# A decoder layer on one core: the state-space tables moved from GpSimd to VectorE, by sums and differences of angles

## The chip, the cores and the metric

The kernel runs on one core of a Trainium2 chip. The metric is device time in microseconds (us) of one execution, as the median of several runs; lower is better. The core has five engines that run their own instruction queues and wait for each other by semaphores: TensorE (PE; PEld is its loading of weights), VectorE (DVE), ScalarE (ACT), GpSimd (POOL) and SyncE (SP), which here only starts transfers from memory.

## What is computed

One layer of a decoder on a sequence of 256 positions and 2048 channels, in float32. Three token mixers run in parallel on one projection `h = x @ W_in`: a diagonal complex state-space model (S5), and two gated linear attentions (GLA and HGRN2). Their outputs are projected up, gated and summed, then comes an output projection, a layer norm, a squared-ReLU MLP with 8192 hidden channels and a second layer norm. The change touches S5 alone:

```python
dt = exp(log_dt); mag = exp(lr * dt)               # 64 groups, 64 states each
abar = mag * (cos(li * dt) + i sin(li * dt))
bu = einsum('bsgc,gpc->bsgp', ug, bbar)            # complex; 16 channels a group
s_t = abar * s_{t-1} + bu_t                        # scan over 256 positions
y = Re(einsum('bsgp,gcp->bsgc', s, c)) + d * ug
```

## The kernel before, in words

**The main stream.** Nearly all work is big matrix products on TensorE. To keep float32 accuracy with a faster operand type, each operand is split into a high part (rounded, by ScalarE, line 129) and a low part (operand minus high part, by VectorE, line 107); a product is then three matmuls, or two where a 256-column operand holds both parts side by side (lines 1341 to 1343, and 1346 and 1347). The weights stream from memory through SP's queue in tiles of 512 KB, 128 partitions by 1024 elements, fetched up to 8 tiles ahead (`AHEAD`). Each tile is split shortly before use: `emit_split` gives ScalarE the high part, `emit_lower` gives VectorE the low part, a 128x1024 subtraction. So TensorE needs one such subtraction for every tile, and a tile lasts two *steps*; a step is six matmuls of 512 columns, or eight of 512 and 256 alternating.

**The side tasks.** All else (S5, the attentions, norms) is written as generators that are woken between steps. The order on each engine is that in which the Python code issues instructions; nothing reorders it later. `run_tasks(vb, sb)` (called at line 1318) is the pacing: every instruction on VectorE or ScalarE issued through the helpers adds its estimated time to a counter, every step takes 1240 ns off, and tasks of lower priority go on only while both counters are negative. `yield n` puts a task to sleep for about 2n steps. GpSimd's instructions are not counted.

**S5.** `s5_params` prepares, for each of 64 groups' states, angle steps, and pages `sn` and `cs` with sine and cosine of fine angles (time 0 to 15) and coarse ones (16 times 0 to 15). The work then goes through 16 *half blocks* of 4 groups, in two pairs of 128 states:
- `s5_prepare` (line 432) sets up, per block of two half blocks, masked copies of B and C (`EB`, `EC`, lines 444 and 445), transposes them on TensorE into `W`, and stacks u and B three times on 96 partitions by transfers on SP (`RU`, `RB`); then ScalarE rounds the stacks to high parts, and VectorE subtracts on the 32 partitions that are to hold low parts.
- `s5_tables` (line 484) makes, for a half block, sine and cosine of all 256 times from fine and coarse angles by the addition theorem: six products or sums of 128x512 on GpSimd (lines 493 to 498).
- `s5_main` (line 502) multiplies the stacks (`pb`, line 519), rotates the result by the tables so that the recurrence becomes real (products that read PSUM, 128x256 each, one per pair and part), scans it (line 543, four scans of 128x256), rotates back, and multiplies by C (line 563).

The attentions (`attention`, line 605) work by levels, each with products on TensorE that need VectorE's last result (line 634). Their two large factors are multiplied once before level 0. GpSimd otherwise only fills one page per attention with zeros and starts small transfers at the beginning.

Of the kernel before, what the change touches and what calls it, by code (L numbers as in the profile page):

```python
# [8 lines left out]
F32 = mybir.dt.float32  # L9
# [46 lines left out]
def trunk_kernel(ctx: ExitStack, tc, io, out):  # L56
# [48 lines left out]
    def tt(o, a, b, op):  # L105
        used["v"] += size(o) / 0.96 + 80
        V.tensor_tensor(o, a, b, op=op)  # L107
# [170 lines left out]
    def s5_params():  # L278
# [153 lines left out]
    def s5_prepare():  # L432


        yield from wait_for("par")
        EB, EC = S5["EB"], S5["EC"]
        b4 = S5["B"].rearrange("q r (j c) -> q r j c", j=32)
        c4 = S5["C"].rearrange("r i (b p) -> r i b p", b=8)
        for b in range(8):
            for g in range(2):  # L440
                h = slice(64 * g, 64 * g + 64)
                for ri in range(2):
                    used["v"] += 120
                    V.tensor_copy(EB[h, ri, :, g, :], b4[h, ri, 4 * b:4 * b + 4, :])
                ts(EC[:, :, g, :], c4[:, :, b, :], S5["gm"][:, g:g + 1], None, ALU.mult)
            yield 4
            yield from wait_for(("u", b // 4))
            yield from room("hf", 1, 4)
            ps = psm()
            transposes(ps, [EB[:, ri].rearrange("q j g c -> q (j g c)") for ri in range(2)] +  # L450
                       [EC[:, ri].rearrange("r g p -> r (g p)") for ri in range(2)])
            W = half((128, 4, 128))
            act(W, ps.rearrange("p (b s) -> p b s", b=4), AF.Copy)
            S5["W", b] = W
            yield 1
            u = uT[b // 4][:, b % 4, :]
            for hb in (2 * b, 2 * b + 1):
                yield from room("hf", 4, 4)
                RU, RB = half((96, 2, 256)), half((96, 2, 256))
                for i in range(2):  # L460
                    r = slice(32 * (2 * (hb % 2) + i), 32 * (2 * (hb % 2) + i) + 32)
                    for k in range(3):
                        nc.sync.dma_start(RU[32 * k:32 * k + 32, i, :], u[r])
                        nc.sync.dma_start(RB[32 * k:32 * k + 32, i, :], W[r, 0:2, :].rearrange("p a b -> p (a b)"))
                yield 3
                SU, SB = half((96, 2, 256), F32R), half((96, 2, 256), F32R)
                act(SU, RU, AF.Copy)
                act(SB, RB, AF.Copy)
# [14 lines left out]

    def s5_tables(hb):

        def fine(x):
            return x[:, 0, 2 * hb:2 * hb + 2, :].unsqueeze(2).to_broadcast([128, 2, 16, 16])

        def coarse(x):
            return x[:, 1, 2 * hb:2 * hb + 2, :].unsqueeze(3).to_broadcast([128, 2, 16, 16])  # L490
        sn, cs = S5["sn"], S5["cs"]
        so, co, w = (half((128, 2, 16, 16)) for _ in range(3))
        G.tensor_tensor(co, coarse(cs), fine(cs), op=ALU.mult)
        G.tensor_tensor(w, coarse(sn), fine(sn), op=ALU.mult)
        G.tensor_tensor(co, co, w, op=ALU.subtract)
        G.tensor_tensor(so, coarse(sn), fine(cs), op=ALU.mult)
        G.tensor_tensor(w, coarse(cs), fine(sn), op=ALU.mult)
        G.tensor_tensor(so, so, w, op=ALU.add)
        free(w)
        S5["tab", hb] = tuple(x.rearrange("p i a b -> p i (a b)") for x in (so, co)), (so, co)  # L500

    def s5_main():
        yps = None
        yield from wait_for("par")
        yield from room("hf", 4)
        s5_tables(0)
        for hb in range(16):
            b, off = hb // 2, 2 * (hb % 2)
            u = uT[b // 4]
            (sn, cs), tabs = S5.pop(("tab", hb))  # L510
            while ("stack", hb) not in S5:
                yield 1
            W = S5["W", b]
            SU, SB = S5.pop(("stack", hb))
            uid[0] += 1
            pb = [psa.tile([128, 2, 256], F32, tag="m2", bufs=2, name=f"pb{uid[0]}_{i}") for i in range(2)]
            for i in range(2):
                for ri in range(2):
                    T.matmul(pb[i][:, ri, :], lhsT=SB[:, i, ri * 128:(ri + 1) * 128], rhs=SU[:, i, :],  # L519
                             start=True, stop=True)  # L520
            free(SU, SB)
            if hb + 1 < 16:
                yield from room("hf", 3, 4)
                s5_tables(hb + 1)
            yield from room("hf", 3, 3)
            zr, zi, w1 = half(), half(), half()
            for i in range(2):
                tt(zr[:, i, :], pb[i][:, 0, :], cs[:, i, :], ALU.mult)
                tt(w1[:, i, :], pb[i][:, 1, :], sn[:, i, :], ALU.mult)
            yield 0  # L530
            tt(zr, zr, w1, ALU.add)
            for i in range(2):
                tt(zi[:, i, :], pb[i][:, 1, :], cs[:, i, :], ALU.mult)
            yield 0
            for i in range(2):
                tt(w1[:, i, :], pb[i][:, 0, :], sn[:, i, :], ALU.mult)
            tt(zi, zi, w1, ALU.subtract)
            yield 0
            for z in (zr, zi):
                for i in range(2):  # L540
                    j = 2 * hb + i
                    used["v"] += 340
                    V.tensor_tensor_scan(z[:, i, :], S5["mag"][:, j:j + 1].to_broadcast([128, 256]),  # L543
                                         z[:, i, :], 0.0, ALU.mult, ALU.add)
# [757 lines left out]
    for s, (c, ku, j, t) in enumerate(steps):  # L1302
# [105 lines left out]
```

## Time and profile before

| | |
|---|---|
| median of 3 runs | 1694.33 us (1694.15 to 1695.88) |
| the profiled execution's own time | 1696.22 us |
| its span, first to last instruction | 1694.4 us |
| busy: PE, DVE, ACT, POOL | 1671.3, 1190.8, 825.5, 161.3 us |
| mean granted clock of TensorE | 0.996 |
| GpSimd's table operations | 96, starting between 75.9 and 699.7 us |
| read from memory | 308.71 MB, 183 GB/s over the span |

How to read the rows that follow: a group's row gives the line of the code, the engine, the operation, the tiles written and read with their shapes (partitions x elements), the count, then busy time in us and the mean duration of one in ns, then idle time of that engine just before them with what ended it. Nearly all VectorE instructions go through one helper at line 107 and ScalarE's through line 129, so they are told apart by tiles and shapes: `pg` is a page of 1024 elements per partition, `hf` a half page of 512, `acc`, `pb` and `m` are PSUM banks. Successive instructions of one engine overlap a little, so a group's busy time over its count is less than the mean duration. A row of the timeline starts with the start and the duration in us; x2 means two instructions in a row, and the duration is that of both. A busy PE includes matmuls whose modelled ends overlap.

### The profile page before, as it was taken

Reading aid. Unit: us, or ns where it says so; the run is one execution under the profiler, and the core shown is the slowest. Engines: PE = TensorE matmul, PEld = TensorE weight load, DVE = VectorE, ACT = ScalarE, POOL = GpSimd, SP = SyncE. Lnnn points to the kernel's source line nnn. Section 1 sums busy time; section 2 is a strip of 40 time slices with the busy share of each in tenths; the row PEclk is TensorE's granted clock in tenths of the full one; section 3 lists DMA queues with packets and bytes.
Section 4 is the critical chain, followed back from the end, with each engine's and each line's share of the span. In section 5 each row is a group of like instructions: output and inputs, shape, how many; then the busy total and the mean of one; then the engine's idle time right before and its main releaser. Section 6 shows DMA issues by size and latency. Waiting matters only on the chain.

```text
span 1694.4 us, 24226 instructions
## 1 busy us (share of the span) xinstructions
PE 1671.3 (99%) x9396; PEld 1386.1 (82%) x9396; DVE 1190.8 (70%) x1587; ACT 825.5 (49%) x1166; POOL 161.3 (10%) x121
## 2 busy tenths in 40 slices
PE   9999999999999999999999999999999999999997
PEld 7887788887877877788888888888888888888886
DVE  6968778797998999985575667545555545555556
ACT  5553554564644434435554466454454545464550
POOL 3222022012332332200000000000000000000000
PEclk9999999999999999999999999999999999999999
DMA  9945655564555665676676545655656565656561
GB/s 287 275 145 157 178 177 168 153 194 139 173 180 169 194 196 172 207 221 186 200 263 220 187 150 150 197 188 187 211 179 206 163 213 171 218 163 208 197 233 50
DMA packets 222900, 318.70 MB, mean 188 GB/s; under 512 B 13205, under 2 KB 122129, under 8 KB 222785
## 3 DMA queue, kind: packets, MB, share of 16 engines
q1 hardware_dynamic: 217488, 308.59, 58.3%
q10 hardware_dynamic: 4528, 7.31, 1.3%
q0 software_dynamic: 768, 1.25, 0.5%
q8 instruction: 74, 1.21, 0.3%
q14 instruction: 42, 0.34, 0.1%
HBM read 308.71 MB, written 2.10 MB: 183 GB/s over the span
## 4 chain that ended last, share of the span: by engine, by line
PE 66%; DVE 4%; issue 1%; ACT 0%; DVEq 0%
PE acc L1341 15%; PE acc L1342 15%; PE acc L1343 15%; PE acc L1346 14%; PE acc L1347 7%; DVE pg L107 2%; DVE hf L107 1%; PE m L134 1%; DVE hf L543 1%; PE m L563 1%; DVE pg L118 0%; PE pb L519 0%; ACT pg L129 0%; DVE st L941 0%; DVEq L1403 0%
## 5 line engine op out<-in xcount | busy, mean ns | idle before, releaser
L129 ACT ACTIVATE pg<-pg 128x1024 fp32r<-128x1024 f32 (+2 forms) x604 | 603.1, 1028 | 413.7 <-PE acc L1342 147.0
L107 DVE TENSOR_TENSOR pg<-pg,pg 128x1024 fp32r<-128x1024 f32 (+3 forms) x646 | 749.9, 1188 | 58.9 <-ACT pg L129 32.7
L1341 PE MATMUL acc<-pg,pg 128*128 128x512 f32 x1504 | 595.5, 396 | 2.7 <-DVE pg L107 1.8
L1342 PE MATMUL acc<-pg,pg 128*128 128x512 f32 x1504 | 587.3, 390 | 2.7 <-DVE pg L107 2.7
L1343 PE MATMUL acc<-pg,pg 128*128 128x512 f32 x1504 | 587.0, 390 | 0.2
L1346 PE MATMUL acc<-pg,pg 128*128 128x512 f32 x1552 | 551.9, 400 | 0.0
L1347 PE MATMUL acc<-pg,pg 128*128 128x256 f32 x1552 | 436.6, 281 | 1.9 <-DVE pg L107 1.9
L1346 PEld LDWEIGHTS acc<-pg,pg 128*128 128x128 f32 x1552 | 292.4, 188 | 72.9 <-issue 0.7
L1341 PEld LDWEIGHTS acc<-pg,pg 128*128 128x128 f32 x1504 | 282.8, 188 | 68.4 <-issue 5.8
L1343 PEld LDWEIGHTS acc<-pg,pg 128*128 128x128 f32 x1504 | 282.6, 188 | 61.5 <-DVE pg L107 1.4
L1342 PEld LDWEIGHTS acc<-pg,pg 128*128 128x128 f32 x1504 | 282.9, 188 | 60.6 <-DVE pg L107 5.1
L1347 PEld LDWEIGHTS acc<-pg,pg 128*128 128x128 f32 x1552 | 293.9, 189 | 2.8 <-DVE pg L107 2.3
L129 ACT ACTIVATE hf<-acc 128x256 f32<-128x256 f32 (+2 forms) x103 | 40.0, 388 | 184.5 <-PE acc L1347 179.6
L107 DVE TENSOR_TENSOR pg<-pg,acc 128x512 f32<-128x512 f32 x56 | 38.3, 685 | 121.3 <-PE acc L1343 121.3
L107 DVE TENSOR_TENSOR hf<-acc,hf 128x256 f32<-128x256 f32 (+1 forms) x69 | 29.1, 421 | 131.9 <-ACT hf L129 131.9
L107 DVE TENSOR_TENSOR hf<-hf,hf 128x512 f32<-128x512 f32 (+1 forms) x144 | 106.6, 758 | 4.7 <-ACT hf L129 2.8
L129 ACT ACTIVATE hf<-hf 128x256 f32<-128x256 f32 (+1 forms) x152 | 67.7, 456 | 2.3 <-DMA hf<-pg 0.5
L129 ACT ACTIVATE pg<-acc 128x512 f32<-128x512 f32 x40 | 23.8, 595 | 83.7 <-PE acc L1343 74.5
L107 DVE TENSOR_TENSOR hf<-pb,hf 128x256 f32<-128x256 f32 x128 | 46.5, 414 | 22.8 <-PE pb L519 16.8
L107 DVE TENSOR_TENSOR pg<-hf,pg 128x256 fp32r<-128x256 f32 x84 | 34.7, 421 | 27.7 <-ACT pg L129 27.6
L129 ACT ACTIVATE pg<-m 128x512 fp32r<-128x512 f32 (+2 forms) x35 | 19.6, 559 | 68.0 <-PE m L134 51.8
L543 DVE TENSOR_TENSOR_SCAN hf<-p,hf 128x256 f32<-128x256 f32 x64 | 47.7, 792 | 0.0
(128 smaller groups left out, 641.1 us busy)
## 6 DMA issues: line engine op xcount, KB each, us to landing
pg<-in_w_in_dram SPq DMA_DIRECT2D x224, 512.0 KB, 4.2
pg<-in_w_mlp_in_dram SPq DMA_DIRECT2D x128, 512.0 KB, 4.6
pg<-in_w_mlp_out_dram SPq DMA_DIRECT2D x128, 512.0 KB, 4.0
pg<-in_w_up_dram SPq DMA_DIRECT2D x48, 512.0 KB, 4.7
pg<-in_w_out_dram SPq DMA_DIRECT2D x32, 512.0 KB, 5.5
pg<-in_s_w_glu_dram SPq DMA_DIRECT2D x8, 512.0 KB, 4.7
hf<-pg SPq DMA_DIRECT2D x96, 32.0 KB, 1.9
hf<-hf SPq DMA_DIRECT2D x96, 32.0 KB, 1.9
```

The costliest lines, as they stand in the source:

```text
L107: V.tensor_tensor(o, a, b, op=op)
L129: S.activation(o, a, f, **kw)
L134: T.transpose(ps[:, i * 128:(i + 1) * 128], s, ident)
L543: V.tensor_tensor_scan(z[:, i, :], S5["mag"][:, j:j + 1].to_broadcast([128, 256]), z[:, i, :], 0.0, ALU.mult, ALU.add)
L563: T.matmul(yps[r, 0:256], lhsT=W[:, 2 + ri, r], rhs=m[:, i, :], start=ri == 0, stop=ri == 1)
L1341: T.matmul(ps, lhsT=a[0][:, sl], rhs=wh[:, i, :], start=f, stop=False)
L1342: T.matmul(ps, lhsT=a[0][:, sl], rhs=wl[:, i, :], start=False, stop=False)
L1343: T.matmul(ps, lhsT=a[1][:, sl], rhs=wh[:, i, :], start=False, stop=l)
L1346: T.matmul(ps, lhsT=wh[:, i, n], rhs=a[2], start=f, stop=False)
L1347: T.matmul(ps[:, 0:256], lhsT=wl[:, i, n], rhs=a[0], start=False, stop=l)
```

## The change

- The time vector's fine part is moved by a half (0.5 to 15.5), and the tables no longer come from all 16 fine angles but from the first 8: with coarse angle c and fine angle f, cos(c ± f) and sin(c ± f) share the same four products, so 8 fine angles give 16 times, 8 by the sum and 8, in reverse order, by the difference. A table now takes four operations of 128x256 (two products, a sum, a difference); sine and cosine together take eight. They are issued on VectorE, through the counted helper, with a `yield 0` after each pair. GpSimd has none of them.
- `pb` holds a part (real or imaginary) of both pairs in one bank rather than both parts of one pair, so each rotation product covers both pairs: four products of 128x512 per half block instead of eight of 128x256.
- u and B are split before they are stacked, on all 128 partitions, once per block: ScalarE rounds u and B to high parts (two copies of 128x256; the copy of C's half shrinks to 128x256), VectorE makes two subtractions of 128x256. The transfers on SP, as many and as large as before, pick the high or low part. The subtractions on 32 partitions are gone.
- The pacing takes 1290 ns off per step instead of 1240.

```diff
+        ts(tvec[:, 0, :], tvec[:, 0, :], 0.5, None, ALU.add)
...
-            yield from room("hf", 1, 4)
+            yield from room("hf", 3, 4)
+            u = uT[b // 4][:, b % 4, :]
+            UP = half((128, 2, 256), F32R)
+            act(UP[:, 0, :], u, AF.Copy)
...
-            W = half((128, 4, 128))
-            act(W, ps.rearrange("p (b s) -> p b s", b=4), AF.Copy)
+            W, BP = half((128, 2, 128)), half((128, 2, 256), F32R)
+            act(BP[:, 0, :], ps[:, 0:256], AF.Copy)
+            act(W, ps[:, 256:512].rearrange("p (b s) -> p b s", b=2), AF.Copy)
             S5["W", b] = W
+            yield 0.5
+            tt(UP[:, 1, :], u, UP[:, 0, :].bitcast(F32), ALU.subtract)
+            tt(BP[:, 1, :], ps[:, 0:256], BP[:, 0, :].bitcast(F32), ALU.subtract)
             yield 1
...
-                        nc.sync.dma_start(RU[32 * k:32 * k + 32, i, :], u[r])
-                        nc.sync.dma_start(RB[32 * k:32 * k + 32, i, :], W[r, 0:2, :].rearrange("p a b -> p (a b)"))
+                        nc.sync.dma_start(RU[32 * k:32 * k + 32, i, :], UP[r, int(k == 1), :].bitcast(F32))
+                        nc.sync.dma_start(RB[32 * k:32 * k + 32, i, :], BP[r, int(k == 2), :].bitcast(F32))
...
-                yield 0.5
-                tt(SU[32:64], RU[32:64], SU[32:64].bitcast(F32), ALU.subtract)
-                tt(SB[64:96], RB[64:96], SB[64:96].bitcast(F32), ALU.subtract)
...
-        so, co, w = (half((128, 2, 16, 16)) for _ in range(3))
-        G.tensor_tensor(co, coarse(cs), fine(cs), op=ALU.mult)
-        G.tensor_tensor(w, coarse(sn), fine(sn), op=ALU.mult)
-        G.tensor_tensor(co, co, w, op=ALU.subtract)
-        G.tensor_tensor(so, coarse(sn), fine(cs), op=ALU.mult)
-        G.tensor_tensor(w, coarse(cs), fine(sn), op=ALU.mult)
-        G.tensor_tensor(so, so, w, op=ALU.add)
-        free(w)
+        so, co = half((128, 2, 16, 16)), half((128, 2, 16, 16))
+        for o, x1, y1, x2, y2, op1, op2 in ((co, cs, cs, sn, sn, ALU.subtract, ALU.add),
+                                            (so, sn, cs, cs, sn, ALU.add, ALU.subtract)):
+            w = half((128, 2, 2, 16, 8))
+            tt(w[:, 0], coarse(x1), fine(y1), ALU.mult)
+            tt(w[:, 1], coarse(x2), fine(y2), ALU.mult)
+            yield 0
+            tt(o[:, :, :, 8:16], w[:, 0], w[:, 1], op1)
+            tt(o[:, :, :, 7::-1], w[:, 0], w[:, 1], op2)
+            free(w)
+            yield 0
...
-                    T.matmul(pb[i][:, ri, :], lhsT=SB[:, i, ri * 128:(ri + 1) * 128], rhs=SU[:, i, :],
+                    T.matmul(pb[ri][:, i, :], lhsT=SB[:, i, ri * 128:(ri + 1) * 128], rhs=SU[:, i, :],
...
-            for i in range(2):
-                tt(zr[:, i, :], pb[i][:, 0, :], cs[:, i, :], ALU.mult)
-                tt(w1[:, i, :], pb[i][:, 1, :], sn[:, i, :], ALU.mult)
+            tt(zr, pb[0], cs, ALU.mult)
+            tt(w1, pb[1], sn, ALU.mult)
...
-        run_tasks(1240, 1240)
+        run_tasks(1290, 1290)
```

The order of VectorE's instructions moves at three places. The first is where the tables of the first half block are made, about 87 to 93 us into the trace. `pg_829`, `pg_859` and, after the change, `pg_835`, `pg_866` and `pg_899` are low parts of successive weight tiles; `s5eb` and `s5ec` are the masked copies for `s5_prepare`; `hf_884` and `hf_911` hold products of sines and cosines, `hf_883` and `hf_882` the two tables. Before:

```order
L107 TENSOR_TENSOR pg_829<-pg_621,pg_828 128x1024
L107 TENSOR_TENSOR pg_733<-acc_765,hf_861 128x256
L444 COPY s5eb<-pg_188 64x4x16 x2
L112 TENSOR_SCALAR s5ec<-pg_189,gmask 128x2x64
L444 COPY s5eb<-pg_188 64x4x16 x2
L112 TENSOR_SCALAR s5ec<-pg_189,gmask 128x2x64
L107 TENSOR_TENSOR pg_859<-pg_651,pg_858 128x1024
```

After:

```order
L445 COPY s5eb<-pg_188 64x4x16 x2
L112 TENSOR_SCALAR s5ec<-pg_189,gmask 128x2x64
L107 TENSOR_TENSOR pg_835<-pg_619,pg_834 128x1024
L107 TENSOR_TENSOR pg_735<-acc_769,hf_868 128x256
L107 TENSOR_TENSOR hf_884<-pg_578 128x256
L107 TENSOR_TENSOR hf_884<-pg_577 128x256
L107 TENSOR_TENSOR hf_883<-hf_884 128x32x8 x2
L107 TENSOR_TENSOR pg_866<-pg_649,pg_865 128x1024
L107 TENSOR_TENSOR hf_911<-pg_577,pg_578 128x256
L107 TENSOR_TENSOR hf_911<-pg_578,pg_577 128x256
L107 TENSOR_TENSOR hf_882<-hf_911 128x32x8 x2
L107 TENSOR_TENSOR pg_899<-pg_675,pg_898 128x1024
```

The masked copies come one weight tile earlier, and one table (four operations) now stands ahead of each of two weight tiles' low parts; `pg_866` is the counterpart of `pg_859`.

The second place is the start of the GLA attention, about 143 to 151 us. `pg_1385`, `pg_1416` and, after, `pg_1398`, `pg_1436` are low parts of weights, `hf_1456` and `hf_1476` the attention's diagonal, and the last row is the product on which level 0 waits (`pg_1287`, `pg_1298`). Before:

```order
L112 TENSOR_SCALAR s5ec<-pg_189,gmask 128x2x64
L107 TENSOR_TENSOR pg_1385<-pg_1133,pg_1384 128x1024
L118 SCALAR_TENSOR_TENSOR pg_1287<-acc_1326,hf_1418 128x256
L107 TENSOR_TENSOR hf_1372<-hf_1372,hf_1232 128x512
L107 TENSOR_TENSOR hf_904<-hf_904,hf_1231 128x512
L107 TENSOR_TENSOR pg_1416<-pg_1165,pg_1415 128x1024
L107 TENSOR_TENSOR hf_1456<-m_1458,dg 128x256
L107 TENSOR_TENSOR pg_1287<-pg_1287,pg_978 128x1024
```

After:

```order
L118 SCALAR_TENSOR_TENSOR hf_883<-hf_883,hf_882 128x512
L107 TENSOR_TENSOR pg_1398<-pg_1147,pg_1397 128x1024
L118 SCALAR_TENSOR_TENSOR pg_1298<-acc_1337,hf_1438 128x256
L107 TENSOR_TENSOR hf_1413<-pg_507,hf_1413 128x256
L107 TENSOR_TENSOR hf_1421<-m_1415,hf_1421 128x256
L107 TENSOR_TENSOR pg_1436<-pg_1205,pg_1435 128x1024
L107 TENSOR_TENSOR hf_1476<-m_1478,dg 128x256
L107 TENSOR_TENSOR pg_1298<-pg_1298,pg_1003 128x1024
```

The rotation back of a half block (two 128x512) has moved ahead, and two new subtractions of a block's u and B (`hf_1413`, `hf_1421`) stand in its place; no table operation is near.

The third is the start of a half block late in S5, where `pb` is read. Before (the last half block):

```order
L107 TENSOR_TENSOR pg_7167<-pg_7040,pg_7166 128x1024
L107 TENSOR_TENSOR hf_7208<-pb_0_7202,hf_6946 128x256
L107 TENSOR_TENSOR hf_7210<-pb_0_7202,hf_6945 128x256
L107 TENSOR_TENSOR hf_7208<-pb_1_7203,hf_6946 128x256
L107 TENSOR_TENSOR hf_7210<-pb_1_7203,hf_6945 128x256
L107 TENSOR_TENSOR hf_7208<-hf_7208,hf_7210 128x512
L107 TENSOR_TENSOR hf_7209<-pb_0_7202,hf_6946 128x256
L107 TENSOR_TENSOR hf_7209<-pb_1_7203,hf_6946 128x256
L107 TENSOR_TENSOR pg_7190<-pg_7042,pg_7189 128x1024
```

After (a half block of the same stretch that makes the next one's tables):

```order
L107 TENSOR_TENSOR hf_5875<-pg_578 128x256
L107 TENSOR_TENSOR hf_5875<-pg_577 128x256
L107 TENSOR_TENSOR hf_5874<-hf_5875 128x32x8 x2
L107 TENSOR_TENSOR pg_5836<-pg_5730,pg_5835 128x1024
L107 TENSOR_TENSOR pg_5839<-m_5890,pg_5838 128x4x128
L107 TENSOR_TENSOR hf_5903<-pg_577,pg_578 128x256
L107 TENSOR_TENSOR hf_5903<-pg_578,pg_577 128x256
L107 TENSOR_TENSOR pg_5888<-pg_5750,pg_5887 128x1024
L107 TENSOR_TENSOR hf_5873<-hf_5903 128x32x8 x2
L107 TENSOR_TENSOR hf_5928<-pb_0_5867,hf_5596 128x512
L107 TENSOR_TENSOR hf_5930<-pb_1_5868,hf_5595 128x512
L107 TENSOR_TENSOR pg_5914<-pg_5773,pg_5913 128x1024
```

The tables' eight operations stand ahead of the first products from `pb`, with weights' low parts between them; the products are fewer and longer. On GpSimd the 96 table operations are gone from the order, and its zero fills and first transfers stay.

More of the change, by code (lines that the diff above doesn't have):

```diff
@@ L451, in s5_prepare @@
                        [EC[:, ri].rearrange("r g p -> r (g p)") for ri in range(2)])
-            W = half((128, 4, 128))
-            act(W, ps.rearrange("p (b s) -> p b s", b=4), AF.Copy)
+            W, BP = half((128, 2, 128)), half((128, 2, 256), F32R)
+            act(BP[:, 0, :], ps[:, 0:256], AF.Copy)
+            act(W, ps[:, 256:512].rearrange("p (b s) -> p b s", b=2), AF.Copy)
             S5["W", b] = W
+            yield 0.5
+            tt(UP[:, 1, :], u, UP[:, 0, :].bitcast(F32), ALU.subtract)
+            tt(BP[:, 1, :], ps[:, 0:256], BP[:, 0, :].bitcast(F32), ALU.subtract)
             yield 1
-            u = uT[b // 4][:, b % 4, :]
             for hb in (2 * b, 2 * b + 1):
@@ L468, in s5_prepare @@
                 act(SB, RB, AF.Copy)
-                yield 0.5
-                tt(SU[32:64], RU[32:64], SU[32:64].bitcast(F32), ALU.subtract)
-                tt(SB[64:96], RB[64:96], SB[64:96].bitcast(F32), ALU.subtract)
                 free(RU, RB)
-                yield 1.5
+                yield 1
                 S5["stack", hb] = SU, SB
+            free(UP, BP)
     SIN2 = 6.2831845
@@ L486, in fine @@
         def fine(x):
-            return x[:, 0, 2 * hb:2 * hb + 2, :].unsqueeze(2).to_broadcast([128, 2, 16, 16])
+            return x[:, 0, 2 * hb:2 * hb + 2, 0:8].unsqueeze(2).to_broadcast([128, 2, 16, 8])
         def coarse(x):
-            return x[:, 1, 2 * hb:2 * hb + 2, :].unsqueeze(3).to_broadcast([128, 2, 16, 16])
+            return x[:, 1, 2 * hb:2 * hb + 2, :].unsqueeze(3).to_broadcast([128, 2, 16, 8])
         sn, cs = S5["sn"], S5["cs"]
-        so, co, w = (half((128, 2, 16, 16)) for _ in range(3))
-        G.tensor_tensor(co, coarse(cs), fine(cs), op=ALU.mult)
-        G.tensor_tensor(w, coarse(sn), fine(sn), op=ALU.mult)
-        G.tensor_tensor(co, co, w, op=ALU.subtract)
-        G.tensor_tensor(so, coarse(sn), fine(cs), op=ALU.mult)
-        G.tensor_tensor(w, coarse(cs), fine(sn), op=ALU.mult)
-        G.tensor_tensor(so, so, w, op=ALU.add)
-        free(w)
+        so, co = half((128, 2, 16, 16)), half((128, 2, 16, 16))
[9 more added lines that the diff above has]
+            yield 0
         S5["tab", hb] = tuple(x.rearrange("p i a b -> p i (a b)") for x in (so, co)), (so, co)
@@ L505, in s5_main @@
         yield from room("hf", 4)
-        s5_tables(0)
+        yield from s5_tables(0)
         for hb in range(16):
@@ L523, in s5_main @@
                 yield from room("hf", 3, 4)
-                s5_tables(hb + 1)
+                yield from s5_tables(hb + 1)
             yield from room("hf", 3, 3)
             zr, zi, w1 = half(), half(), half()
-            for i in range(2):
-                tt(zr[:, i, :], pb[i][:, 0, :], cs[:, i, :], ALU.mult)
-                tt(w1[:, i, :], pb[i][:, 1, :], sn[:, i, :], ALU.mult)
+            tt(zr, pb[0], cs, ALU.mult)
+            tt(w1, pb[1], sn, ALU.mult)
             yield 0
             tt(zr, zr, w1, ALU.add)
-            for i in range(2):
-                tt(zi[:, i, :], pb[i][:, 1, :], cs[:, i, :], ALU.mult)
+            tt(zi, pb[1], cs, ALU.mult)
             yield 0
-            for i in range(2):
-                tt(w1[:, i, :], pb[i][:, 0, :], sn[:, i, :], ALU.mult)
+            tt(w1, pb[0], sn, ALU.mult)
             tt(zi, zi, w1, ALU.subtract)
@@ L562, in s5_main @@
                 for ri, m in ((0, sre), (1, cs)):
-                    T.matmul(yps[r, 0:256], lhsT=W[:, 2 + ri, r], rhs=m[:, i, :],
+                    T.matmul(yps[r, 0:256], lhsT=W[:, ri, r], rhs=m[:, i, :],
                              start=ri == 0, stop=ri == 1)
```

## The prediction

> **What bounds the kernel now.** I read the page's first part, then busy time by stage, then PE's idle gaps with what ended them, then VectorE's and GpSimd's rows around those gaps.
>
> ```profile
> span 1694.4 us, 24226 instructions
> PE 1671.3 (99%) x9396; PEld 1386.1 (82%) x9396; DVE 1190.8 (70%) x1587; ACT 825.5 (49%) x1166; POOL 161.3 (10%) x121
> ```
>
> TensorE is the bound: 1671.3 of 1694.4 us. The change gives TensorE no less work, so all it can win is where PE waits. In the stages of 50 us below the columns are length, then busy us (and instructions) of PE, PEld, DVE, ACT, POOL, then the granted clock.
>
> ```profile
> 50.00:100.00 50.00, 48.07 (x261) 40.79 (x261) 44.17 (x56) 20.99 (x29) 18.71 (x12) 0.97 0.73 214
> 100.00:150.00 50.00, 47.93 (x322) 40.51 (x320) 38.74 (x53) 30.68 (x38) 10.18 (x8) 1.00 0.53 167
> 150.00:200.00 50.00, 48.98 (x559) 38.99 (x560) 35.75 (x55) 19.80 (x27) 0.00 (x0) 0.97 0.54 159
> 500.00:550.00 50.00, 48.39 (x221) 38.04 (x220) 45.32 (x60) 21.82 (x23) 14.20 (x9) 1.00 0.58 173
> 600.00:650.00 50.00, 48.13 (x223) 38.39 (x222) 45.46 (x63) 21.11 (x24) 12.63 (x9) 1.00 0.51 155
> ```
>
> PE's idle time here is 1.93 + 2.07 + 1.02 = 5.02 us early and 1.61 + 1.87 = 3.48 us in two late stages. Everything the change touches runs between about 60 and 760 us. The two early gaps also cost clock. The next rows are four stretches of 3.41 us in the same columns: for each early gap the one that holds it and the one after.
>
> ```profile
> 89.74:93.15 3.41, 1.48 (x9) 1.03 (x8) 3.40 (x5) 0.41 (x1) 1.60 (x2) 1.00 0.00 0
> 93.15:96.56 3.41, 3.41 (x13) 2.93 (x12) 3.41 (x5) 0.00 (x0) 2.39 (x1) 0.50 0.48 130
> 147.76:151.17 3.41, 0.43 (x20) 0.16 (x21) 3.41 (x4) 0.00 (x0) 2.12 (x1) 1.00 0.32 77
> 151.17:154.58 3.41, 3.41 (x70) 2.88 (x64) 3.41 (x6) 0.00 (x0) 0.00 (x0) 0.50 0.61 171
> ```
>
> After each gap TensorE runs 3.41 us at clock 0.50, which loses 1.7 us: 3.4 us for both. So at most 5.02 + 3.48 + 3.4 = 11.9 us is to be had.
>
> **Who makes PE wait.** The first gap: PE's row with the idle time before it, then VectorE's (start, duration); the last row, from elsewhere, is a measure:
>
> ```profile
> 92.69 0.39 PE L1347 MATMUL acc<-pg,pg 128*128 128x256 f32 x1 [1.93 <-DVE pg L107]
> 87.83 0.28 DVE L444 COPY s5eb<-pg 64x64 f32<-64x64 f32 x2
> 88.03 1.10 DVE L112 TENSOR_SCALAR s5ec<-pg,gmask 128x128 f32<-128x128 f32 x1
> 89.14 1.08 DVE L444 COPY s5eb<-pg 64x64 f32<-64x64 f32 x2
> 90.23 1.26 DVE L112 TENSOR_SCALAR s5ec<-pg,gmask 128x128 f32<-128x128 f32 x1
> 91.42 2.35 DVE L107 TENSOR_TENSOR pg<-pg,pg 128x1024 fp32r<-128x1024 f32 x2
> 142.94 0.29 DVE L112 TENSOR_SCALAR s5ec<-pg,gmask 128x128 f32<-128x128 f32 x1
> ```
>
> PE waits for the low part of a weight tile (the 128x1024 subtraction). VectorE reaches it late because the small operations ahead of it ran beside GpSimd's tables: TENSOR_SCALAR 1.10 and 1.26 us against 0.29 alone (142.94), the pair of copies 1.08 against 0.28. That is 0.81 + 0.97 + 0.80 = 2.6 us. The second gap has the same shape:
>
> ```profile
> 139.35 1.11 DVE L444 COPY s5eb<-pg 64x64 f32<-64x64 f32 x2
> 140.38 1.08 DVE L112 TENSOR_SCALAR s5ec<-pg,gmask 128x128 f32<-128x128 f32 x1
> 141.48 1.44 DVE L444 COPY s5eb<-pg 64x64 f32<-64x64 f32 x2
> 144.61 2.15 DVE L107 TENSOR_TENSOR hf<-hf,hf 128x512 f32<-128x512 f32 x2
> 146.68 2.08 DVE L107 TENSOR_TENSOR pg<-pg,pg 128x1024 fp32r<-128x1024 f32 x1
> 151.01 0.98 PE L634 MATMUL m<-pg,pg 128*32 128x16 f32 x64 [2.98 <-DVE pg L107]
> ```
>
> Against the same measures the copies and the s5ec operation lost 0.83 + 0.79 + 1.16 = 2.8 us, the pair of 512-element products 0.8 (2.15 where two at the late 0.66, worked out below, take 1.3) and the subtraction 0.9 (2.08 against 1.19): 4.5 us for a gap of 2.98. The longest gap of the late stage:
>
> ```profile
> 631.03 3.18 DVE L543 TENSOR_TENSOR_SCAN hf<-p,hf 128x256 f32<-128x256 f32 x2
> 636.59 0.50 PE L1342 MATMUL acc<-pg,pg 128*128 128x512 f32 x1 [1.87 <-DVE pg L107]
> ```
>
> Two scans took 3.18 us beside GpSimd; two at the late 0.63 us (below) take 1.3: 1.9 us, the whole gap.
>
> **The change, part by part, on VectorE.** The groups by shape (count | busy us, mean ns | idle before), first of 60 to 745 us, where GpSimd works, with one of ScalarE, then of 745 to 1640, where GpSimd does nothing:
>
> ```profile
> L107 DVE TENSOR_TENSOR pg<-pg,pg 128x1024 fp32r<-128x1024 f32 x218 | 281.7, 1304 | 2.1 <-ACT pg L129 1.7
> L107 DVE TENSOR_TENSOR hf<-hf,hf 128x512 f32<-128x512 f32 x105 | 78.7, 772 | 0.9
> L543 DVE TENSOR_TENSOR_SCAN hf<-p,hf 128x256 f32<-128x256 f32 x60 | 45.2, 800 | 0.0
> L107 DVE TENSOR_TENSOR hf<-pb,hf 128x256 f32<-128x256 f32 x123 | 44.7, 414 | 22.8 <-PE pb L519 16.8 <-issue 6.0
> L107 DVE TENSOR_TENSOR hf<-hf,hf 32x512 fp32r<-32x512 f32 x32 | 23.3, 730 | 3.7 <-ACT hf L129 2.8
> L129 ACT ACTIVATE hf<-acc 128x256 f32<-128x256 f32 x28 | 10.7, 382 | 50.3 <-PE acc L1347 49.5
> ```
> ```profile
> L107 DVE TENSOR_TENSOR pg<-pg,pg 128x1024 fp32r<-128x1024 f32 x323 | 383.8, 1220 | 29.2 <-ACT pg L129 24.3 <-PE acc L1342 2.9 <-issue 0.9
> L107 DVE TENSOR_TENSOR pg<-pg,acc 128x512 f32<-128x512 f32 x47 | 32.2, 685 | 107.0 <-PE acc L1343 107.0
> L107 DVE TENSOR_TENSOR hf<-hf,hf 128x512 f32<-128x512 f32 x7 | 4.6, 683 | 0.1
> L543 DVE TENSOR_TENSOR_SCAN hf<-p,hf 128x256 f32<-128x256 f32 x4 | 2.5, 676 | 0.0
> L107 DVE TENSOR_TENSOR hf<-pb,hf 128x256 f32<-128x256 f32 x7 | 2.6, 416 | 0.0
> ```
>
> *GpSimd's tables go.* By busy time, 218 subtractions cost 281.7 − 218 × 383.8/323 = 22.7 us more than late ones, 105 products 78.7 − 105 × 4.6/7 = 9.7, 60 scans 45.2 − 60 × 2.5/4 = 7.7: VectorE gets back 40.1 us; the other groups, the s5ec and s5eb ones above among them, come on top. Products that read PSUM keep their time (414 and 416 ns), so it is two SBUF operands that collide.
>
> The Trainium skill (SBUF — State Buffer, Who interferes with whom) says that a VectorE instruction with two SBUF inputs, or a copy or tensor_scalar in a two-port mode, locks against a GpSimd instruction that reads SBUF, and the loser blocks for the other's whole length. The rows agree in kind (PSUM products untouched, 0.29 us drawn out to 1.1); a loss of all GpSimd time would by this page exceed the 40.1 us that the groups show, and the groups decide.
>
> *Tables on VectorE:* 8 operations of 128x256 per half block, 128 in all. Nearest row: the 128x256 products, 44.7/123 = 0.363 us back to back, 46.5 us; alone 0.414 each, 53.0. I take 46.5, since they stand in pairs. *Rotations:* 128 of 128x256 (46.5 us) become 64 of 128x512 reading PSUM, 64 × 0.685 = 43.8: −2.7. *Low parts of u and B:* 32 of 32x512 (23.3 us) become 16 of 128x256 (5.8): −17.5. The added half step on the time vector is one operation on 16 columns, nothing.
>
> Net on VectorE: 46.5 − 40.1 − 2.7 − 17.5 = −13.8 us. The bounds are +32.8 (tables at 53.0 and nothing given back: 53.0 − 2.7 − 17.5) and −29 (the 16 s5ec operations giving back 0.97 each, 15.5 more).
>
> *Others.* ScalarE gets three copies of 128x256 for one of 128x512 in each of 8 blocks, at most 24 × 0.382 = 9.2 us over 700, and is busy 49% of the time: hidden. If it were full, that would be the price. SP issues the same 192 stack transfers, now behind VectorE's subtraction instead of ScalarE's copy, and weight loads queue behind them on SP; those are issued up to 8 tiles ahead, two steps each, so a wait of a step or two is hidden. Without that cover PE would wait for a tile. PE's matmuls are the same in number and size.
>
> *At the gaps.* First: the order puts half the tables (4 × 0.363 = 1.5 us) ahead of the subtraction that was late. The small operations alone give back 2.6, so 1.1 of 1.93 us; the rest has to come from the work before 87 us, which ran beside another set of GpSimd's products:
>
> ```profile
> 80.97 2.08 DVE L107 TENSOR_TENSOR pg<-pg,pg 128x1024 fp32r<-128x1024 f32 x1
> 83.31 2.92 DVE L107 TENSOR_TENSOR pg<-pg,hf 128x512 f32<-128x512 f32 x2
> ```
>
> These two rows give back 0.9 and 1.6 us more (2.08 against 1.19, 2.92 against 1.3). I take the gap as gone. Second: by the order no table operation stands near the late product, only the two new subtractions of a block (2 × 0.363 = 0.7 us); 4.5 − 0.7 = 3.8 us come back for 2.98. Gone. With both gaps the 3.4 us of half clock go: 5.02 + 3.4 = 8.4. Late stage: the causes go, but 8 × 0.363 = 2.9 us of tables stand at each half block's start and the task budget per step rises from 1240 to 1290 ns, so I take three quarters of 3.48, 2.6. Sum: 8.4 + 2.6 = 11.0 us.
>
> The profiled execution took 1696.22 us, its span 1694.4; from it 1685.2. It is 1.89 above the median of the runs, so for the median 1694.33 − 11.0 = **1683.3 us**.
>
> **Rivals.**
> 1. *VectorE becomes the bound* (slower). If GpSimd gives nothing back, VectorE gets 32.8 us more over 16 half blocks, 2.05 each. From 450 to 700 it has 18.06 us idle:
>
> ```profile
> 450.00:700.00 250.00, 246.17 (x1131) 196.47 (x1130) 231.94 (x311) 112.52 (x128) 70.43 (x48) 1.00 0.59 186
> ```
>
> Some 8 half blocks fall there, 16.4 us: it would be full, its idle time now being waits for others, and PE would wait for most of it: 1694.3 + 16.4 = 1710.7. It decides where less than 32.8 us come back; 40.1 are shown. Chance 0.04.
> 2. *The half clock stays.* If the two slow stretches come by themselves, only 11.0 − 3.4 = 7.6 is won: 1686.7. Against it: in both cases the stretch just before had PE busy 1.48 and 0.43 of 3.41 us. Chance 0.10. The Trainium skill (TensorE: Matmul & The Clock Gate, Part 1) has the clock halve after an idle window of about 3.4 us; by that rule gaps of 1.93 and 2.98 would be too short, and this rival's 1686.7 would hold. The trace speaks against the rule's length.
> 3. *The waits move.* Tables and first products stand together at each half block's start, 8 × 0.363 + 4 × 0.685 = 5.6 us where 2.9 stood. If that costs PE a microsecond in each of 8 half blocks, the late stage loses 8 instead of 3.5: 1694.3 − 8.4 + 4.5 = 1690.4. Against: the code yields after each pair. Chance 0.14.
> 4. *One early gap stays*, because the tables eat what the collision gave back: 2.98 + 1.7 less, 1688.0. Chance 0.08. That the change doesn't do what it says is excluded for GpSimd, on which the order has no product left; that its products have nothing to do with PE's waits, about 1694: 0.02.
>
> **The numbers.** My forecast has 0.62. A fifth of a per cent, 3.4 us, is what a measurement can tell from no change: below 1690.9 counts as faster. Faster: 0.62 + 0.10 + 0.08 + half of rival 3 = 0.87; within: 0.09; slower 0.04. The range runs from 1680.0 (all 11.9 us, 1682.4, less some 2 us of spread as between profile and median) to 1690.4, rival 3; rival 1 and the last are left out.
>
> **What would show it.** No GpSimd products; the 128x1024 subtraction near 1.19 us of busy time and scans near 0.63 before 745; PE idle below 1 us from 50 to 200 and clock 1.00 throughout; VectorE busy below 605 us from 60 to 760. A gap of over 1 us at PE ended by VectorE in 50 to 700, or a 0.50 clock there, proves a step wrong; a VectorE busy over 47 of 50 us for several stages means rival 1 or 3.

## The result, and the profile after

The changed kernel takes 1682.84 us (median of 4 runs, 1682.36 to 1683.05), the kernel before in the same session 1695.11: a ratio of 0.9924, 95% interval 0.991 to 0.9937. The forecast was 1683.3. The profiled execution took 1682.36 us against 1696.22, 13.9 less. Most executions of the kernel before took about 1694.3 us with a mean granted clock of 0.997, or about 1696.1 us with 0.996. The page of after:

```profile
span 1680.6 us, 24111 instructions
PE 1665.3 (99%) x9396; PEld 1384.1 (82%) x9396; DVE 1159.6 (69%) x1636; ACT 828.8 (49%) x1183; POOL 15.6 (1%) x25
```

By stage (length, then busy us and instructions of PE, PEld, DVE, ACT, POOL, then the clock), the five stages shown of before and the two long ones:

```profile
50.00:100.00 50.00, 50.00 (x284) 42.90 (x283) 40.95 (x68) 23.75 (x34) 0.00 (x0) 1.00 0.72 212
100.00:150.00 50.00, 48.60 (x445) 41.38 (x445) 40.45 (x64) 31.18 (x40) 0.96 (x1) 1.00 0.63 191
150.00:200.00 50.00, 50.00 (x448) 39.97 (x448) 40.62 (x61) 22.83 (x29) 0.00 (x0) 1.00 0.60 172
500.00:550.00 50.00, 50.00 (x233) 40.09 (x232) 46.34 (x73) 23.95 (x28) 0.00 (x0) 1.00 0.57 167
600.00:650.00 50.00, 50.00 (x231) 40.05 (x230) 43.86 (x66) 21.42 (x25) 0.00 (x0) 1.00 0.65 202
450.00:700.00 250.00, 250.00 (x1152) 201.70 (x1151) 221.88 (x337) 115.39 (x140) 0.00 (x0) 1.00 0.62 189
60.00:760.00 700.00, 698.60 (x4622) 572.05 (x4621) 579.94 (x902) 346.60 (x481) 2.89 (x3) 1.00 0.60 181
```

PE's idle time from 50 to 200 us went from 5.02 to 1.40, in the late stages to nothing, and the granted clock is 1.00 throughout these rows. VectorE is busy 579.9 of 700 us instead of 605.4, though it does the tables now. Its groups from 60 to 745 us (count | busy us, mean ns | idle before):

```profile
L107 DVE TENSOR_TENSOR pg<-pg,pg 128x1024 fp32r<-128x1024 f32 x223 | 269.3, 1217 | 4.7 <-ACT pg L129 2.8 <-issue 1.9
L107 DVE TENSOR_TENSOR hf<-hf,hf 128x512 f32<-128x512 f32 x109 | 72.0, 684 | 0.8
L107 DVE TENSOR_TENSOR hf<-pb,hf 128x512 f32<-128x512 f32 x64 | 42.4, 683 | 7.8 <-PE pb L528 7.8
L549 DVE TENSOR_TENSOR_SCAN hf<-p,hf 128x256 f32<-128x256 f32 x64 | 39.4, 671 | 0.0
L107 DVE TENSOR_TENSOR hf<-hf 128x256 f32<-128x256 f32 x64 | 24.3, 421 | 0.6
L107 DVE TENSOR_TENSOR hf<-pg,pg 128x256 f32<-128x256 f32 x32 | 12.1, 418 | 0.0
L107 DVE TENSOR_TENSOR hf<-pg 128x256 f32<-128x256 f32 x32 | 12.0, 417 | 0.0
L445 DVE COPY s5eb<-pg 64x64 f32<-64x64 f32 x32 | 4.6, 184 | 0.1
L112 DVE TENSOR_SCALAR s5ec<-pg,gmask 128x128 f32<-128x128 f32 x16 | 4.5, 279 | 0.1
```

The large groups with two SBUF operands are back at the durations that the kernel before has only after 745 us: subtractions 1217 ns (1304 before the change), scans 671 (800), products 684 (772). The tables are the three rows of 128x256: 48.4 us.

From 50 to 760 us one wait of PE is left, in the first products of the state-space part. Its row comes first, then ScalarE's rows before it; the last two rows are the same copies and the same products in the kernel before:

```profile
113.05 0.74 PE L528 MATMUL pb<-hf,hf 96*128 96x256 f32 x4 [1.40 <-ACT hf L129]
108.66 1.28 ACT L129 ACT_TABLE_LOAD   x1
109.95 2.01 ACT L129 ACTIVATE pg<-pg 128x1024 f32<-128x1024 f32 x2
111.86 1.14 ACT L129 ACTIVATE hf<-hf 96x512 fp32r<-96x512 f32 x2
115.79 1.14 ACT L129 ACTIVATE hf<-hf 96x512 fp32r<-96x512 f32 x2
120.95 0.64 PE L519 MATMUL pb<-hf,hf 96*128 96x256 f32 x4
```

The copies that round the stacks (111.86) stand on ScalarE behind two long activations of the attention's decay and a table load ahead of these, and PE waits for the copies. In the kernel before the copies ran as late, but the products came 5.2 us after the copies' start, not 1.2. The change took the two subtractions between them out, and with them half of the sleep: `yield 0.5` and `yield 1.5` became one `yield 1`.

### The profile page after: what moved, and what is told of

The parts are those of the page before. It is cut to its first block, busy times and chain, and to the rows that moved or that the text cites. A ratio compares the mean times of both kernels' runs of the same rounds, so it can differ in the third digit from the quotient of the medians.

```text
span 1680.6 us, 24111 instructions
## 1 busy us (share of the span) xinstructions
PE 1665.3 (99%) x9396; PEld 1384.1 (82%) x9396; DVE 1159.6 (69%) x1636; ACT 828.8 (49%) x1183; POOL 15.6 (1%) x25
## 4 chain that ended last, share of the span: by engine, by line
PE 97%; DVE 1%; DMA 1%; ACT 0%; SPq 0%; issue 0%; DVEq 0%; ACTq 0%
PE acc L1352 21%; PE acc L1347 21%; PE acc L1349 20%; PE acc L1348 20%; PE acc L1353 11%; PE m L134 1%; PE m L569 1%; PE m L640 1%; PE pb L528 0%; DVE pg L107 0%; DMA pg<-in_w_in_dram 0%; DVE pg L118 0%; PE m L697 0%; PE m L696 0%; PE m L694 0%; PE m L651 0%
## 5 line engine op out<-in xcount | busy, mean ns | idle before, releaser
L107 DVE TENSOR_TENSOR pg<-pg,pg 128x1024 fp32r<-128x1024 f32 (+2 forms) x646 | 729.6, 1155 | 61.3 <-ACT pg L129 33.3
L107 DVE TENSOR_TENSOR hf<-hf,hf 128x512 f32<-128x512 f32 x112 | 74.0, 684 | 0.8
L107 DVE TENSOR_TENSOR pg<-m,pg 128x512 fp32r<-128x512 f32 (+1 forms) x34 | 23.4, 689 | 37.5 <-ACT pg L129 20.4
L107 DVE TENSOR_TENSOR hf<-pb,hf 128x512 f32<-128x512 f32 x64 | 42.4, 683 | 7.8 <-PE pb L528 7.8
```

## The experiments

Theory A: the time came from GpSimd's products colliding with VectorE's operations on two SBUF operands. Theory B: it came from VectorE having less to do in rotations and splits, and from the faster pacing. All ratios below are to the kernel before, in the same session on the same chip.

**The tables alone** on the kernel before:

```diff
-        G.tensor_tensor(co, coarse(cs), fine(cs), op=ALU.mult)
...
+            V.tensor_tensor(w[:, 0], coarse(x1), fine(y1), op=ALU.mult)
+            V.tensor_tensor(w[:, 1], coarse(x2), fine(y2), op=ALU.mult)
+            yield 0
+            V.tensor_tensor(o[:, :, :, 8:16], w[:, 0], w[:, 1], op=op1)
+            V.tensor_tensor(o[:, :, :, 7::-1], w[:, 0], w[:, 1], op=op2)
```

> The kernel before with the new tables alone: eight operations of 128x256 on VectorE per half block, not counted by the pacing, which stays at 1240; rotations, stacks and splits as before. Theory A (the time came from GpSimd's products colliding with VectorE's operations on two SBUF operands): the collision goes, VectorE gains 48.4 us of tables and gets about 56 us back, so the long waits go: 1684 to 1687 us, PE idle from 50 to 200 below 2 us, clock 1.00, 128x1024 subtractions near 1.21 us of busy time each before 745 us. Theory B (the time came from less VectorE work in rotations and splits, 25 us, and from the faster pacing): neither is here and VectorE's own work grows, so 1693 to 1700 us.

1685.64 us, ratio 0.9938 (0.9922 to 0.9953): 10.2 of the 12.3 us. As A has it, although VectorE has more work of its own, without the collision, than in either kernel. Its subtractions from 60 to 745 us, and three long stages:

```profile
L107 DVE TENSOR_TENSOR pg<-pg,pg 128x1024 fp32r<-128x1024 f32 x222 | 268.4, 1218 | 1.3 <-ACT pg L129 0.8
```
```profile
50.00:200.00 150.00, 149.91 (x1180) 125.04 (x1180) 119.54 (x196) 76.58 (x98) 0.96 (x1) 1.00 0.63 189
200.00:450.00 250.00, 248.49 (x2075) 204.58 (x2074) 208.91 (x352) 130.10 (x210) 1.91 (x2) 1.00 0.56 167
450.00:700.00 250.00, 248.07 (x1141) 199.42 (x1140) 232.21 (x376) 111.52 (x128) 0.00 (x0) 1.00 0.61 188
```

The collision is gone (1218 ns), and with it the early waits: PE loses 0.09 us from 50 to 200 where it lost 5.02, and the clock is 1.00. From 200 to 700 us it still loses 1.51 + 1.93 = 3.44 us, hardly less than the 3.83 before, though elsewhere: before, nothing was lost up to 450. VectorE is as full late as it was before the change, 232.2 and 231.9 of 250 us. So the tables alone won their time early; late, PE waited about as long with the tables on VectorE as it had with the collision. In the changed kernel, with merged rotations, early splits and its own pacing, VectorE is busy 221.9 us late, and these last waits are absent; those parts were not tried one by one.

**The tables back on GpSimd**, all else as changed:

```diff
-            tt(w[:, 0], coarse(x1), fine(y1), ALU.mult)
...
+        G.tensor_tensor(co, coarse(cs), fine(cs), op=ALU.mult)
+        G.tensor_tensor(w, coarse(sn), fine(sn), op=ALU.mult)
+        G.tensor_tensor(co, co, w, op=ALU.subtract)
...
```

> The changed kernel with the six products of 128x512 per half block back on GpSimd, all else as changed (rotations over both pairs, early splits, pacing 1290). Theory A: the collision is back, 128x1024 subtractions at 1.29 us of busy time each before 745 us against 1.21; waits of PE come back in part, since VectorE has 20 us less other work than before: 1688 to 1694 us. Theory B: the gain stays, 1681 to 1685 us, since VectorE is relieved of 48 us of tables as well.

1706.37 us, ratio 1.0059 (1.004 to 1.0079). B falls, and A's number was far too low: although VectorE has 20 us less of other work, this kernel is 11 us slower than the one before. Its subtractions from 60 to 745 us, and the two stages:

```profile
L107 DVE TENSOR_TENSOR pg<-pg,pg 128x1024 fp32r<-128x1024 f32 x216 | 292.7, 1368 | 6.5 <-issue 4.4 <-ACT pg L129 2.1
```
```profile
200.00:450.00 250.00, 243.33 (x2044) 201.38 (x2043) 210.48 (x294) 126.97 (x211) 53.58 (x33) 1.00 0.56 167
450.00:700.00 250.00, 240.88 (x1101) 192.43 (x1100) 222.43 (x261) 110.24 (x133) 75.13 (x42) 0.99 0.58 176
```

PE loses 6.7 + 9.1 us where the kernel before lost 0 and 3.8. What made it worse is asked below.

**Idle products on GpSimd**, added to the changed kernel, so that VectorE's own work and order stay. They add work that nothing uses:

```diff
+        w4 = wz.rearrange("p (a b) -> p a b", a=16)
+        for k in range(12):
+            G.tensor_tensor(w4, so[:, k % 2], co[:, k % 2], op=ALU.mult)
```

> The changed kernel with twelve products of 128x256 per half block added on GpSimd, reading the new tables and writing a page that nothing uses. VectorE's own work and order are those of the changed kernel. Theory A: 128x1024 subtractions near 1.29 us of busy time each before 745 us, scans near 0.75, PE waits for VectorE again: 1688 to 1698 us. Theory B, or a collision that costs VectorE but not PE: 1682 to 1684 us.

**Idle fills**, the same place, work that nothing uses and that reads next to nothing (one element per partition, to hold the fills to their half block):

```diff
+        G.tensor_tensor(wz[:, 0:1], so[:, 1, 15, 0:1], co[:, 1, 15, 0:1], op=ALU.mult)
+        for k in range(24):
+            G.memset(wz, 0.0)
```

> The changed kernel with 24 fills of 128x256 with zeros per half block added on GpSimd, which write SBUF and read none of it, of about the same length in all as the idle products. If two readers collide, as theory A has it: VectorE's groups as in the changed kernel (1.21 us, scans 0.62) and 1682 to 1684 us. If any work of GpSimd in SBUF is in VectorE's way: as the idle products, 1688 us or more.

The products: 1699.57 us, ratio 1.0024 (1.0015 to 1.0034). The fills: 1683.11 us, 0.9922 (0.9904 to 0.994), the changed kernel's own time. VectorE's rows from 60 to 745 us, with idle products and then with fills:

```profile
L107 DVE TENSOR_TENSOR pg<-pg,pg 128x1024 fp32r<-128x1024 f32 x216 | 279.8, 1304 | 2.6 <-issue 1.9 <-ACT pg L129 0.8
L552 DVE TENSOR_TENSOR_SCAN hf<-p,hf 128x256 f32<-128x256 f32 x60 | 56.6, 996 | 0.0
L107 DVE TENSOR_TENSOR hf<-pb,hf 128x512 f32<-128x512 f32 x60 | 39.6, 681 | 0.3 <-PE pb L531 0.3
L112 DVE TENSOR_SCALAR s5ec<-pg,gmask 128x128 f32<-128x128 f32 x16 | 9.8, 615 | 0.1
```
```profile
L107 DVE TENSOR_TENSOR pg<-pg,pg 128x1024 fp32r<-128x1024 f32 x223 | 269.4, 1217 | 4.7 <-ACT pg L129 2.9 <-issue 1.9
L552 DVE TENSOR_TENSOR_SCAN hf<-p,hf 128x256 f32<-128x256 f32 x64 | 39.4, 671 | 0.0
L112 DVE TENSOR_SCALAR s5ec<-pg,gmask 128x128 f32<-128x128 f32 x16 | 5.2, 324 | 0.1
450.00:700.00 250.00, 250.00 (x1151) 201.67 (x1151) 222.37 (x337) 115.79 (x139) 62.41 (x200) 1.00 0.62 189
```

Products that feed nothing cost 16.5 us more than fills, which keep GpSimd busy 62 of 250 us late and cost nothing. The fills came out shorter than the products: from 60 to 760 us GpSimd was busy 130 us with fills, 225 with products and 148 with the tables of the kernel before. VectorE's waits for GpSimd don't show among its idle times; its operations themselves take longer. This is the collision by itself: scans 996 ns against 671, subtractions 1304 against 1217, products from PSUM unchanged. Fills draw out only the small one-input operations (s5ec 324 against 279 ns). The Trainium skill (SBUF — State Buffer, Who interferes with whom) has a VectorE instruction with two SBUF inputs contend with a GpSimd instruction that reads SBUF and not with one that only writes it, and copies and tensor_scalar in two-port modes contend with either; these rows agree, except that they don't show in which mode the copies and s5ec operations ran.

**The pacing.** Why was the kernel with the tables back slower than the one before? Two theories: P, that the faster pacing overfills VectorE, and Q, that the new order hurts. First the kernel with the tables back:

```diff
-        run_tasks(1290, 1290)
+        run_tasks(1240, 1240)
```

> The kernel with the tables back on GpSimd, but paced at 1240 as before the change instead of 1290. Theory P (the faster pacing fills VectorE to the brim, and with the collision on top it overflows): most of the 1706 goes, 1688 to 1695 us, PE idle from 200 to 700 below 8 us against 15.8. Rival Q (the order of the early splits and long rotations is what hurts beside GpSimd): 1702 to 1708 us.

Then the kernel before:

```diff
-        run_tasks(1240, 1240)
+        run_tasks(1290, 1290)
```

> The kernel before with one number changed, the pacing from 1240 to 1290. Theory P: slower than before, 1699 to 1707 us, with VectorE over 47 of 50 us in several stages from 450 to 700. Rival Q: within 2 us of before.

And the changed kernel:

```diff
-        run_tasks(1290, 1290)
+        run_tasks(1260, 1260)
```

> The changed kernel with the pacing at 1260 instead of 1290. If pacing only matters where VectorE is near full, that is with the collision: 1682 to 1684 us. If the faster pacing is itself part of the gain: 1685 us or more.

With the tables back and 1240: 1695.62 us, ratio 1.0003 (0.9993 to 1.0012), just above P's range. The profile fell on the longest of its ten runs, 1698.69 us; there 8.6 us of PE's time are lost from 200 to 700 where under 8 was expected and 15.8 stood at 1290. The kernel before at 1290: 1706.67 us, ratio 1.0066 (1.0051 to 1.0081). P holds: the pacing alone costs 11 us where GpSimd collides. Q isn't excluded as a smaller part: at 1240 the kernel with the tables back is no faster than the one before, though VectorE has less to do in it, and from 450 to 700 us PE loses 7.41 us against 3.83. Without the collision the changed kernel at 1260 took 1680.7 us, ratio 0.9912 (0.9895 to 0.9928), below all that was expected; so pacing has a price there too, 2 us. The kernel with the tables back at 1240, the kernel before at 1290, then the changed one at 1260:

```profile
450.00:700.00 250.00, 242.59 (x1092) 193.02 (x1091) 233.96 (x271) 110.44 (x133) 79.38 (x45) 0.98 0.56 176
```
```profile
450.00:700.00 250.00, 244.36 (x1124) 194.63 (x1123) 238.74 (x324) 114.86 (x135) 71.04 (x47) 1.00 0.58 182
```
```profile
50.00:200.00 150.00, 150.00 (x1181) 125.27 (x1180) 117.48 (x184) 79.21 (x104) 0.96 (x1) 1.00 0.63 193
60.00:760.00 700.00, 700.00 (x4625) 574.05 (x4624) 573.93 (x889) 347.36 (x481) 2.87 (x3) 1.00 0.60 182
```

(The last two rows are of the repeat below.) At 1290 the kernel before has VectorE busy 238.7 of 250 us, against 231.9 at 1240; and the changed kernel at 1260 has no gap of PE left from 50 to 760.

**Which pacing is best**, all on one chip, 4 or 5 runs each; at 1240 the changed kernel's state-space part is not issued to its end when the products that use it come, so 1240 is left out.

> The changed kernel once more, paced at 1290, to stand beside the two slower pacings on one chip: 1682 to 1684 us.

> The changed kernel paced at 1260 once more. If the two microseconds that it won are real (no wait of ScalarE's stack copies at about 112 us, and fewer short waits where VectorE was fuller): 1679 to 1681.5 us, all runs below those of the changed kernel. If they were chance: 1682 to 1684 us.

> The changed kernel paced at 1250, the slowest that still lets the state-space part end before the products that need it. If less filling is better all the way: 1679 to 1681 us. If the late end of that part makes TensorE wait at the GLU, about 1000 us: over 1683 us.

At 1290: 1682.88 us (1682.60 to 1683.69). At 1260: 1680.46 (1679.69 to 1681.88), ratio to before 0.9914 (0.99 to 0.9927). At 1250: 1680.72 (1679.97 to 1680.98), 0.9913 (0.99 to 0.9927). No run at 1260 or 1250 was as slow as the fastest at 1290, though the intervals of the ratios overlap. So the changed kernel is some 2 us faster at 1260 than at 1290, and no different at 1250; 1.4 of it is ScalarE's wait at 113 us, which isn't there any more.

**When the clock halves.** Rival 2 left open whether the half clock belongs to the waits. Bursts on VectorE, work that nothing uses, make PE wait in the MLP:

```diff
+        if s in bursts:
+            h = half((128, 512))
+            V.memset(h, 1.0)
+            for _ in range(bursts[s]):
+                V.tensor_tensor(h, h, h, op=ALU.mult)
```

> The changed kernel with twelve bursts of products of 128x512 on VectorE (14 to 28 in a row, on a page that nothing uses), 36 steps apart in the MLP, where VectorE is otherwise half idle, so that PE waits 0 to some 8 us after each. Theory W (the clock is granted by fixed stretches of 3.41 us: one in which PE is busy under about 0.46 is followed by one at half clock, whatever the length of the wait): half clock after each stretch below 0.44, none above 0.50, so that a wait of 2 us may halve it and one of 3 us may not. Rival L (a wait must be longer than about 3.4 us): half clock after every wait over 3.4 us and none below. The time is longer by the waits and 1.7 us for each stretch at half clock.

A single run: 1745.25 us. The 12 bursts made 11 waits of over 0.6 us; after the nine of 1.8 us and more the clock halved, after those of 0.63 and 1.28 it did not. The kernel took 62 us longer, less than the 70 that the expectation's sum would give (44.5 us of waits and 15 stretches at half clock at 1.7 us); some of these stretches lay within the waits themselves. Below are rows of stretches of 3.41 us, laid out in steps of 3.41 us from a change of the clock. They are of the bursts, of the kernel with the tables back at 1240, and of the same at 1290:

```profile
1178.13:1181.55 3.42, 0.68 (x4) 0.22 (x2) 3.32 (x6) 1.06 (x1) 0.00 (x0) 1.00 0.69 204
1181.55:1184.96 3.41, 3.33 (x8) 2.66 (x9) 3.41 (x5) 1.06 (x1) 0.00 (x0) 0.50 0.04 14
```
```profile
571.92:575.34 3.42, 1.36 (x7) 0.83 (x6) 3.42 (x7) 0.00 (x0) 0.28 (x1) 1.00 0.00 0
575.34:578.75 3.41, 3.41 (x9) 2.64 (x9) 3.38 (x8) 1.51 (x2) 0.00 (x0) 0.50 0.76 221
```
```profile
387.68:391.10 3.42, 1.72 (x8) 1.10 (x6) 3.42 (x4) 0.47 (x1) 3.42 (x3) 1.00 0.58 153
391.10:394.51 3.41, 1.87 (x69) 1.67 (x70) 3.41 (x2) 0.58 (x1) 2.55 (x2) 1.00 0.00 1
394.51:397.92 3.41, 3.41 (x51) 2.59 (x51) 3.41 (x6) 1.06 (x1) 0.00 (x0) 1.00 0.54 158
```

A wait of 2.06 us that fell into one stretch (PE busy 1.36 of 3.41) halved the next; one of 3.24 us that fell across two (1.72 and 1.87) halved none. Theory W holds, with the border not sharp: stretches with PE busy 0.46 (the kernel before at 1290) and 0.48 of the time (the tables back at 1290) kept the clock, one of 0.47 in the bursts lost it. Rival L falls: seven waits of under 3.4 us were followed by half clock, two in the kernel before, two with the tables back at 1240 and three in the bursts.

## Why the prediction was right, point by point

The total came out within 0.5 us of the forecast, and the main cause was where it was put. That it came so close is partly luck: for the profiled execution the same sum gave 1685.2 us, and 1682.36 was measured, a gain of 13.9 us for 11.0. The median 1694.33, from which the forecast took the same 11.0, lies 1.89 below the profiled execution. Executions that short have a mean clock of 0.997 against 0.996, which fits one halved stretch (1.7 us) instead of two, though no trace of one is kept. Then half of the 3.4 us of clock was not there to win from the median, and gains without a term made up for it.

- *GpSimd's collision is what made PE wait.* Shown: tables alone took 10.2 of 12.3 us, idle products cost 16.5 us, idle fills none. The tables alone end the early waits; late it takes the rest of the change as well.
- *The early gaps.* Forecast 5.02 + 3.4 us of half clock. PE's idle time fell by 3.6, since a new wait of 1.40 us came in; the prediction's own sign, PE idle below 1 us from 50 to 200, is missed by it. The half clock went wholly. At the first gap, the copies and s5ec operations take 1.1 us (82.71 to 83.80) where they took 3.7 (87.83 to 91.49), and the subtraction that was late, with a table ahead of it, ends at 87.9 instead of 92.6:

```profile
82.71 0.28 DVE L445 COPY s5eb<-pg 64x64 f32<-64x64 f32 x2
83.51 0.29 DVE L112 TENSOR_SCALAR s5ec<-pg,gmask 128x128 f32<-128x128 f32 x1
85.97 0.76 DVE L107 TENSOR_TENSOR hf<-hf 128x256 f32<-128x256 f32 x2
86.65 1.22 DVE L107 TENSOR_TENSOR pg<-pg,pg 128x1024 fp32r<-128x1024 f32 x1
```

- *The late stage.* Forecast 2.6 of 3.48; all of it went, and the 0.36 of the stages not quoted then. The reason given, that the causes go with the collision, carries only part of it: without the collision, but with the tables on VectorE and nothing else changed, PE lost 3.44 us from 200 to 700.
- *ScalarE: hidden.* This step failed at one place. On average ScalarE is half idle, but at 112 us the stacks' copies stood behind a table load and two long activations, 1.40 us of PE's time. They are not the extra copies that the forecast priced: the kernel before has them too. What the forecast left out is that the products now follow them after half the sleep. That this is the whole cause was not tried by itself; pacing at 1260 removes the wait.
- *VectorE's sum.* Tables 48.4 us for 46.5, rotations 42.4 for 43.8. The collision gave back 281.7/218 − 269.3/223 = 0.084 us on each of 218 subtractions, 18.4, where the forecast had 22.7 by comparison with late ones; 9.3 on the products (9.7) and 8.3 on the scans (7.7). The groups left aside gave the rest: s5ec 3.7 (8.2 to 4.5), s5eb 3.0 (7.6 to 4.6), and smaller groups with two SBUF operands. In all VectorE's busy time fell by 25.5 us, for −13.8 forecast, inside the bounds.
- *What the gaps don't hold.* From the span's 13.8 us, 3.6 early, 3.8 late, 3.4 of clock and 0.4 in the first 50 us are 11.2. The other 2.6 is in PE's busy time (1671.3 to 1665.3, of which the clock is 3.4). Waits too short for the profile to list as idle would explain it, but no view shows them. The forecast had no term for them.
- *Rival 1* would have needed less than 32.8 us to come back; the five groups above alone gave 42.7. *Rival 2* (half clock stays) was put at 0.10 and fell: it left with the waits. The Trainium skill (TensorE: Matmul & The Clock Gate, Part 1) has the half clock come after an idle window of about 3.4 us. The length, against which the forecast took the trace to speak, agrees with the 3.41 us of the stretches here, but a stretch need not be idle throughout: PE busy 0.44 of it was low enough. *Rival 3* (the waits move) fell in the changed kernel, where PE is busy 250.00 of 250 us late. With the tables alone it came true in part: 1.51 us of waits appeared from 200 to 450, where there had been none. The forecast gave the faster pacing only a share of the quarter that it held back late. Without the collision that pacing cost some 2 us, with it 11.

## What to carry to other kernels

An engine that is off the critical path can cost time through another's operands: look for one group of instructions whose duration grows while a third engine runs, and price the wait at that place, not the average. For the large products and scans here it decided whether the helper reads SBUF or only writes it, and whether the other instruction has one SBUF operand or two. Moving the helper's work to the engine that it disturbed is a trade: here the early waits went at once, the late ones only when that engine was relieved as well. A pacing constant tuned with such a collision has to be tuned again without it, and a fuller VectorE was dear here above all where something stretched its work (11 us against 2).

## What the runs showed of the hardware

- With GpSimd reading SBUF, VectorE's scans went from 671 to 996 ns on average, products with a PSUM operand from 683 to 681. With GpSimd almost only writing, subtractions and scans kept their 1217 and 671 ns, and only small one-input operations were drawn out (s5ec 279 to 324, s5eb 184 to 246 ns).
- The clock is granted for stretches of 3.41 us. At full clock, every stretch seen here with PE busy 0.44 of the time or less was followed by one at half, every one of 0.50 or more by one at full; between 0.46 and 0.48 both occurred. At half clock more is needed to get back:

```profile
1396.58:1400.00 3.42, 0.00 (x0) 0.00 (x0) 3.28 (x6) 0.00 (x0) 0.00 (x0) 1.00 0.00 0
1400.00:1403.41 3.41, 2.14 (x7) 1.85 (x8) 3.41 (x5) 0.00 (x0) 0.00 (x0) 0.50 0.00 0
1403.41:1406.83 3.42, 3.42 (x13) 2.94 (x12) 3.42 (x7) 2.69 (x7) 0.00 (x0) 0.50 0.50 153
```

A stretch at half clock with PE busy 2.14 of 3.41 was followed by another at half, and so was one of 2.37 with the tables back at 1240. This rests on a few stretches of two runs, and what exactly is counted stays open.
